# All values first, the linear projections as pairs of quarter sums, and pooling as the fill of the attention

## The chip, the cores and the metric

The kernel runs on one core of one Trainium2 chip. The core's engines are TensorE (PE, matrix products; PEld is its loading of weights), VectorE (DVE), ScalarE (ACT), GpSimd (POOL) and SyncE (SP, which here issues the DMA transfers). Each engine works through a queue of its own in order and waits on semaphores for the others. SBUF is the memory from which they read, PSUM the memory into which PE writes. The metric is the device time of one execution in microseconds: a median of several runs. One further execution is recorded by the profiler, and its own time is the span.

## The reference

One layer of a hybrid block on a sequence of 1024 tokens of width 1024, led by 16 meta tokens, all in float32. Shortened:

```
u  = rmsnorm(h, norm_mix)                          # h: 16 meta tokens + 1024 tokens
a, q, k, v, r, lr, ga, gb = split(u @ w_in)        # 512, 256, 256, 512, 512, 16, 1024, 1024 columns
p   = for group g of 4 (128 columns each): trailing mean of a over 2, 4, 8, 16 tokens, minus a
y_a = ((p @ w_pool_mix, group by group) * pool_scale) @ w_pool_out
log_a = log_sigmoid(lr @ w_gate_up + b_gate) / 16
o   = gla_chunked(q / 8, k, v, log_a)              # 4 heads, keys of 64, values of 128, chunks of 64 tokens:
      scores[t, s] = sum_k q[t,k] k[s,k] exp(-|b[t,k] - b[s,k]|)   # b: running sum of log_a in the chunk
      o = scores @ v + (q * exp(b)) @ S            # S: state, decayed and added to, chunk by chunk
y_b = (rmsnorm(o, gla_norm) * silu(r)) @ w_gla_out
m   = sigmoid(ga) * y_a + sigmoid(gb) * y_b
h   = h + m @ w_out
h   = h + square(relu(rmsnorm(h) @ w_ff1)) @ w_ff2          # 1024 -> 4096 -> 1024
out = rmsnorm(h)[16:]
```

## The kernel before, in words

A product of two float32 matrices is made of three matmuls on rounded parts (type fp32r): each operand is split into a high part (ACT copies it) and a low part (the operand minus its high part, on DVE or POOL); `mm3` then adds high x high, high x low and low x high into one PSUM bank (lines L250, L251, L252). The normed tokens lie transposed, channels over the 128 partitions, in the high parts `TH` and the low parts `TL`, one array per half of the tokens (512 each, the first with the 16 meta tokens). They are filled in the start stage: eight tiles of 128 tokens are loaded, normed, transposed by PE (L238) and split, and PE also forms each tile's values v for the first two heads, 24 matmuls of 256 or 272 columns a tile.

A block of 128 columns of w_in is projected as 8 x 3 matmuls for each half of the tokens (`project`): 48 matmuls of 512 columns a block, 96 for two; a and k also need the meta tokens, and so three pieces, 72 matmuls. Its weights come by the ring `W1`: a raw load, a high part by ACT (L75), a low part (L76) by DVE, or in the attention by POOL; two blocks are held.

After the start, a table in the code sets an order of pooling and gate blocks: a blocks (`a_block`), mix groups (`mix_block`: DVE forms the running sums `s`, L458 and L461, splits them into `ph`, ACT L464 and DVE L465; PE multiplies them by the mixing weights `mw`; ACT L470 and DVE L471 scale and split the result into `pm`), gate blocks of ga, and four `ya_block`s (pm times w_pool_out, times the gate, to DRAM). A gate needs a logarithmic sigmoid: three ACT passes L479 to L481, DVE L482, and one more ACT pass.

Then `gla`, the attention, runs four units (two pairs of heads x two halves of the tokens). Each unit has an inner part, `inside` (log decay; then six levels, at each of which DVE and ACT grow the decayed keys and queries, L744 to L748, PE makes 64x64 scores, L712, and DVE copies a part of them under a mask, L775), and an outer part, `across` (states L801 and L807, outputs L814 and L824, the norm L833 to L838, PE's transposes L842, gating by r and splitting into `yg` L843 to L846). Both are generators that yield how long PE would have to wait; `pour` spends that time, multiplied by `PACE`, on the fill: blocks of wide matmuls for k, q, the values of the second two heads (`v_second`), r, gb, and w_gla_out on half 0 (`yb_block(j, 0)`). So PE's instructions alternate between small attention matmuls and wide fill, in an order that is written down when the program is made. DVE, ACT, POOL and SP are ordered by a scheduler, which may move an instruction within its engine but not past what it depends on.

After the attention come yb of half 1, the product with w_out, the first MLP layer, and the second. The first MLP layer already computes a pair of two blocks by seven products of quarters (two halves of the tokens x two halves of the channels) where eight would be the plain way: sums and differences of quarters are formed on DVE ahead of the products and behind them. Memory is two stacks, `left` and `right`; what lies over another array's memory must wait for that array's last reader.

Of the kernel before, what the change touches and what calls it, by code (L numbers as in the profile page):

```python
# [31 lines left out]
PACE, LEVEL = 1.62, 1.6  # L32
# [24 lines left out]
class Ring:  # L57


    def __init__(self, nc, raw, hi, lo, depth):  # L60
        self.nc, self.raw, self.hi, self.lo, self.depth = nc, raw, hi, lo, depth
        self.queue, self.loaded, self.done = [], 0, 0
        self.views = {}
        self.eng = nc.vector

    def top_up(self):
        while self.loaded < min(self.done + self.depth, len(self.queue)):
            ap = self.queue[self.loaded]
            s = self.loaded % self.depth
# [34 lines left out]
def kernel(  # L104
# [45 lines left out]
    r_dram = dp.tile([HEADS, 2, P, HALF], F32, name="r_dram")  # L150
    h_dram = dp.tile([8, P, D], F32, name="h_dram")
# [5 lines left out]
    small = left.push("small", [P, 152], F32)  # L157
    small_at = [0]

    def tiny(n):  # L160
        a = small_at[0]
        small_at[0] += n
        assert small_at[0] <= 152
        return small[:, a : a + n]
# [7 lines left out]
    lrT_meta = left.push("lrT_meta", [16, 16], F32)  # L172
# [9 lines left out]
    MH, ML = ([a.rearrange("p k c -> p (k c)")[:, : KT * HALF].rearrange("p (k c) -> p k c", k=KT) for a in t] for t in (TH, TL))  # L182
# [47 lines left out]
    def transposed(u, half, at, tags=("ms",), to=None):  # L230
        rows = u.shape[0]
        th, tl = (t[half] for t in to or (TH, TL))
        if rows == P:
            for j in range(2):
# [4 lines left out]
                split_from_psum(th[:, 4 * j : 4 * j + 4, at : at + P], tl[:, 4 * j : 4 * j + 4, at : at + P], b)  # L239
        else:  # L240
# [38 lines left out]
    def enqueue(steps):  # L279
        for ring, aps, _ in steps:  # L280
            if ring:
# [23 lines left out]
    def buffer(key, depth, size=HALF):  # L305
        S[key] = left.push(key, [P, depth, size], F32)
# [25 lines left out]
    def v_tile(i, t):  # L332
# [16 lines left out]
        else:  # L349
            act.activation(S["v"][i][:, t], b[:, :256], ACT.Copy)  # L350
# [13 lines left out]
    S["v"] = [left.push("v0", [P, NC, 2 * P], F32)]  # L364
    left0 = left.mark()

    def start():
# [8 lines left out]
        S["vw"] = [right.push("vw0", [P, 2, KT, VP], F32R)]  # L376
# [5 lines left out]
        for t in range(8):  # L382
# [9 lines left out]
            if t == 0:  # L392
# [11 lines left out]
        v_tile(0, 7)  # L404
# [13 lines left out]
    def pool_open():  # L418
        left.pop_to(left0)
        buffer("a", 2, SEQ + META)  # L420
        buffer("s", 2, SEQ + META)
        right.pop_to(0)
        S["vw"].append(right.push("vw1", [P, 2, KT, 256], F32R))
        S["pm"] = right.push("pm", [P, 2, 4, SEQ], F32R)
        S["ph"] = right.push("ph", [P, 2, SEQ], F32R)
        mw = S["mw"] = right.push("mw", [P, 2, 4, P], F32R)
        r = raw.load(w_pool_mix.rearrange("g c e -> c g e"), 4 * P).rearrange("p (g e) -> p g e", g=4)
        act.activation(mw[:, 0], r, ACT.Copy)
        pool.tensor_tensor(mw[:, 1], r, f32(mw[:, 0]), ALU.subtract)
        buffer("t1", 2)  # L430
        buffer("g", 6)
        buffer("o", 2)
        raw.lend(left.push("raw2", [P, D], F32))

    step(one, pool_open)
# [3 lines left out]
    def a_block(g):  # L439
# [9 lines left out]
        return fn  # L449

    def mix_block(g):
        def fn():
# [13 lines left out]
            for tag, c in zip(("ms", "sc"), halves()):  # L466
                b = bank(tag)
# [4 lines left out]
                yield  # L472
# [3 lines left out]
    def sigmoid(b):  # L476

        t = nxt("t1")
        act.activation(t, b, ACT.Abs)  # L479
        act.activation(t, t, ACT.Exp, scale=-1.0)  # L480
        act.activation(t, t, ACT.Ln, bias=1.0)  # L481
        dve.scalar_tensor_tensor(t, b, 0.0, t, ALU.min, ALU.subtract)  # L482
        return t

    gates = {}

    def ga_block(d):
        def evac(b, half, at, n):
            t = sigmoid(b)
            g = gates[d, half] = nxt("g")  # L490
            act.activation(g, t, ACT.Exp)

# [863 lines left out]
```

## Time and profile before

| what | value |
| --- | --- |
| median of 3 runs | 1275.84 us (1275.65 to 1278.02) |
| span of the profiled execution | 1273.1 us, 2.7 us below the median |
| PE busy | 1237.9 us, 97% |
| DVE busy | 763.8 us, 60% |
| ACT busy | 592.5 us, 47% |
| POOL busy | 88.0 us, 7% |
| DMA | 164.92 MB, mean 130 GB/s |
| start stage | 0 to 57.9 us |
| pooling and gate blocks | 57.9 to 240.8 us |
| attention with fill | 240.8 to 520.7 us |
| rest (yb of half 1, output product, MLP) | 520.7 to 1273.1 us |

The stages are cut where PE starts on the first instruction of the next. A busy share is an average over stages with different limits; for what a change in one stage is worth the stage itself is looked at. Matmuls overlap in PE, so the mean duration of one in a row of the profile is longer than the distance from one to the next; the distance is had from a stretch of time and the number of matmuls in it. An idle time of an engine is put down to what it waited for last.

### The profile page before, as it was taken

The numbers are of one execution on the slowest core, as the hardware profiler recorded it, in microseconds if no ns is written. First come the engines' busy times: TensorE is split into PE (matmuls) and PEld (weight loads), VectorE is DVE, ScalarE is ACT, GpSimd is POOL, SyncE is SP. The second block draws the span as 40 slices with busy tenths as digits, with TensorE's granted clock in tenths as the row PEclk, the third lists the DMA queues.
The fourth block names the chain that finished last, engine by engine and source line by source line (L and its number), as shares of the span: only waits on it lengthen the run. The fifth ranks groups of instructions, "written<-read, shape, count | busy, mean of one in ns | idle before, by whom it ended". The sixth has DMA issues, their size and how long they took to land.

```text
span 1273.1 us, 17984 instructions
## 1 busy us (share of the span) xinstructions
PE 1237.9 (97%) x6895; PEld 1019.3 (80%) x6895; DVE 763.8 (60%) x1265; ACT 592.5 (47%) x1029; POOL 88.0 (7%) x48
## 2 busy tenths in 40 slices
PE   5999999999999999999999999999999999999997
PEld 4988888888778788778878888888878788888776
DVE  6446222251456554652787766766774877887686
ACT  6334334342465654431665545545553444444544
POOL 1000001000111112720000000000000000000000
PEclk9999999999999999999999999999999999999999
DMA  7111223210123324880235444445469863333532
GB/s 238 49 33 50 83 80 104 66 34 17 51 84 92 111 82 157 292 277 35 84 109 164 149 144 162 149 143 164 157 209 360 286 233 107 97 93 90 170 90 89
DMA packets 138103, 164.92 MB, mean 130 GB/s; under 512 B 10368, under 2 KB 82832, under 8 KB 138016
## 3 DMA queue, kind: packets, MB, share of 16 engines
q1 hardware_dynamic: 138016, 163.76, 40.1%
q8 instruction: 54, 0.88, 0.3%
q14 instruction: 33, 0.27, 0.1%
HBM read 115.50 MB, written 48.23 MB: 129 GB/s over the span
## 4 chain that ended last, share of the span: by engine, by line
PE 87%; DVE 5%; DMA 3%; ACT 2%; POOL 1%; issue 1%; SPq 0%; ACTq 0%; DVEq 0%
PE b_mm L250 13%; PE b_mm L251 13%; PE b_mm L252 13%; PE b_o L252 8%; PE b_o L251 8%; PE b_o L250 8%; PE b_y L250 3%; PE b_y L252 3%; PE b_y L251 3%; PE b_sc L250 2%; PE b_sc L252 2%; PE b_z L250 2%; PE b_sc L251 2%; PE b_z L252 2%; PE b_z L251 2%; PE b_sc L712 1%
## 5 line engine op out<-in xcount | busy, mean ns | idle before, releaser
L250 PE MATMUL b_mm<-th,w1h 128*128 128x512 f32 (+1 forms) x496 | 187.8, 379 | 0.0
L251 PE MATMUL b_mm<-tl,w1h 128*128 128x512 f32 (+1 forms) x496 | 185.0, 373 | 0.0
L252 PE MATMUL b_mm<-th,w1l 128*128 128x512 f32 (+1 forms) x496 | 184.4, 372 | 0.0
L250 PEld LDWEIGHTS b_mm<-th,w1h 128*128 128x128 f32 x496 | 93.4, 188 | 20.7 <-issue 3.4
L252 PEld LDWEIGHTS b_mm<-th,w1l 128*128 128x128 f32 x496 | 93.7, 189 | 16.9
L251 PEld LDWEIGHTS b_mm<-tl,w1h 128*128 128x128 f32 x496 | 93.5, 189 | 15.5
L75 ACT ACTIVATE w1h<-raw 128x1024 fp32r<-128x1024 f32 x40 | 42.4, 1059 | 87.6 <-PE b_mm L251 79.3
L482 DVE SCALAR_TENSOR_TENSOR t<-b_mm,t 128x512 f32<-128x512 f32 x40 | 27.6, 689 | 87.1 <-ACT t L481 87.1
L250 PE MATMUL b_o<-w1h 128*128 128x512 f32 x192 | 75.2, 392 | 2.7 <-DVE h L1179 1.7
L251 PE MATMUL b_o<-w1l,w1h 128*128 128x512 f32 x192 | 75.0, 391 | 1.2 <-DVE w1l L1033 1.2
L252 PE MATMUL b_o<-w1h,w1l 128*128 128x512 f32 x192 | 75.0, 391 | 0.1
L1032 ACT ACTIVATE w1h<-raw 128x512 fp32r<-128x512 f32 x88 | 54.7, 624 | 43.7 <-PE b_sc L251 14.1
L76 POOL TENSOR_TENSOR w1l<-raw,w1h 128x1024 fp32r<-128x1024 f32 x22 | 53.5, 2432 | 269.5 <-ACT w1h L75 269.5
L1033 DVE TENSOR_TENSOR w1l<-raw,w1h 128x512 fp32r<-128x512 f32 x88 | 60.2, 684 | 11.9 <-ACT w1h L1032 11.9
L1227 DVE TENSOR_TENSOR bt<-w,w 128x512 f32<-128x512 f32 x80 | 54.7, 684 | 2.4 <-DMA w<-in_w_ff_dram 2.4
L1032 ACT ACTIVATE w1h<-bt 128x512 fp32r<-128x512 f32 x45 | 28.3, 630 | 57.1 <-issue 33.5
L76 DVE TENSOR_TENSOR w1l<-raw,w1h 128x1024 fp32r<-128x1024 f32 x18 | 22.7, 1260 | 52.7 <-ACT w1h L75 52.2
L251 PE MATMUL b_mm<-wo,th 128*128 128x512 f32 x128 | 50.1, 391 | 1.3 <-DVE wo L913 1.3
L250 PE MATMUL b_sc<-th,w1h 128*128 128x512 f32 x128 | 50.5, 394 | 0.8 <-ACT u2p L1151 0.8
L250 PE MATMUL b_mm<-wo,th 128*128 128x512 f32 x128 | 50.7, 396 | 0.4 <-ACT wo L912 0.4
L251 PE MATMUL b_o<-fxl,fxh 128*128 128x512 f32 x128 | 50.0, 391 | 0.7 <-DVE small L211 0.7
L251 PE MATMUL b_z<-tl,w1h 128*128 128x512 f32 x128 | 49.9, 390 | 0.4 <-DVE tl L975 0.4
(294 smaller groups left out, 3073.6 us busy)
## 6 DMA issues: line engine op xcount, KB each, us to landing
hf_dram<-h SPq DMA_DIRECT2D x112, 256.0 KB, 2.1
raw<-hf_dram SPq DMA_DIRECT2D x112, 256.0 KB, 2.7
raw<-in_w_in_dram SPq DMA_DIRECT2D x32, 512.0 KB, 4.2
w<-in_w_ff_dram SPq DMA_DIRECT2D x64, 256.0 KB, 5.0
rawx<-in_w_ff_dram SPq DMA_DIRECT2D x16, 512.0 KB, 4.3
raw<-in_w_ff_dram SPq DMA_DIRECT2D x16, 512.0 KB, 4.1
xs<-in_x_dram SPq DMA_DIRECT2D x8, 512.0 KB, 5.7
ma_dram<-o SPq DMA_DIRECT2D x16, 256.0 KB, 2.0
```

The costliest lines, as they stand in the source:

```text
L75: self.nc.scalar.activation(hi, raw, ACT.Copy)
L76: self.eng.tensor_tensor(lo, raw, hi.bitcast(F32), ALU.subtract)
L250: pe.matmul(ps, ah, bh, start=first and i == 0, stop=False, skip_group_check=more)
L251: pe.matmul(ps, ah, bl, start=False, stop=False, skip_group_check=more)
L252: pe.matmul(ps, al, bh, start=False, stop=last and i == n - 1, skip_group_check=more)
L482: dve.scalar_tensor_tensor(t, b, 0.0, t, ALU.min, ALU.subtract)
L712: pe.matmul(b[to, e, j], kk[r, s], qq[r, s], start=True, stop=True, tile_position=(e * CH, u * CH))
L1032: act.activation(hi, a, ACT.Copy)
L1033: dve.tensor_tensor(lo, a, f32(hi), ALU.subtract)
L1227: dve.tensor_tensor(bt, w, S["w2"][q[3:]][:, i], ALU.add if q[2] == "+" else ALU.subtract)
```

## The change

*Start.* The weights of all four heads' values are loaded in the start stage, and both halves of the values are formed there, tile by tile, and written to DRAM (`v_dram`). ACT copies each transposed tile once more, in plain float32, into `xr`.

*k and the quarter sums.* `proj_open` forms from `xr` the four sums and differences of input quarters that the seven products need (DVE, one on POOL), and splits them. Meanwhile PE does the two k blocks, whose results go to DRAM.

*Pairs.* q (one pair of blocks), r (two), gb (four) and ga (four) are computed in one stage, `pairs_of_projections`, 11 pairs of seven products with 12 matmuls each, by the functions that the first MLP layer uses (`sums_order`, `sums_weights`, `split`: renamed and moved up). All results go to DRAM.

*Attention.* `gla` begins after that, with the first 10 us of fill poured in ahead of it (`OPENING`) and a `PACE` of 1.0. Its fill is now the pooling branch: four a blocks, four mix groups, four ya blocks, and, as before, yb on half 0. The a blocks are the last readers of `TH` and `TL`; `pm`, `ph`, the sums `s` and `mw` lie over these. k, q, v, r and the gates are read back from DRAM. `across` waits, where the order is made, until the mix groups are written down ("yg"), and a yb block of half 0 until that half's outputs are.

What follows the attention is as before. Lines of the changed kernel are numbered differently: `mm3` is L256 to L258, the sums L712 and L715, the split L719 and L725, the growth of keys and queries L910 and L912, the scores L880, the masked copies L941, the outputs L978 and L988, the norm's transposes L1006.

```diff
-PACE, LEVEL = 1.62, 1.6
+PACE, LEVEL, OPENING = 1.0, 1.6, 10.0
...
+                c = half * HALF + at - OFF[half]
+                act.activation(S["xr"][:, 4 * j : 4 * j + 4, c : c + P], b, ACT.Copy)
...
-            act.activation(S["v"][i][:, t], b[:, :256], ACT.Copy)
+            o = nxt("vo")
+            act.activation(o, b[:, :256], ACT.Copy)
+            nc.sync.dma_start(v_dram[i, t], o)
...
+                load_vw(1)
...
+            if t > 0:
+                v_tile(1, t - 1)
         transposed(um, 0, 0)
+        v_tile(0, 7)
+        v_tile(1, 7)
...
+    def proj_open():
+
+        left.pop_to(base)
+        right.pop_to(1)
+        S["t"] = [tuple(left.push(f"t{i}{k}", [P, 4, HALF], F32R) for k in "hl") for i in range(4)]
+        buffer("t1", 2)
+        buffer("o", 3)
+        piece = lambda half, j: S["xr"][:, 4 * j : 4 * j + 4, half * HALF : (half + 1) * HALF]
+        b11, b21, b12, b22 = (piece(h, j) for h in range(2) for j in range(2))
+
+        def parts(i, a, eng=dve):
+            hi, lo = S["t"][i]
+            act.activation(hi, a, ACT.Copy)
+            eng.tensor_tensor(lo, a, f32(hi), ALU.subtract)
+
+        dve.tensor_tensor(b11, b12, b11, ALU.subtract)
+        parts(0, b11)
+        pool.tensor_tensor(b12, b22, b12, ALU.subtract)
+        dve.tensor_tensor(b22, b22, b11, ALU.subtract)
+        parts(1, b22)
+        dve.tensor_tensor(b21, b21, b22, ALU.subtract)
+        parts(2, b12, pool)
+        parts(3, b21)
+
+    step(one, proj_open)
...
+    PAIRS = [(c + 2 * i * P, put, 2 * i) for c, n, put in (
+        (C_Q, 1, put_q), (C_R, 2, put_r), (C_GB, 4, put_gate(gb_dram)), (C_GA, 4, put_gate(ga_dram)),
+    ) for i in range(n)]
...
+    def pairs_of_projections():
+        load = lambda i, u: load_block(w_in, i, u, PAIRS[i][0])
...
+        plain = lambda half, j: tuple(t[half][:, 4 * j : 4 * j + 4, OFF[half] : OFF[half] + HALF] for t in (TH, TL))
+        x = {"P1": plain(0, 0), "P2": plain(0, 1), "P5": S["t"][0], "P3": plain(1, 1)}
+        x.update(zip(("P6", "P7", "P4"), S["t"][1:]))
+        xb, zb = {}, {}
+        left_over = 7 * len(PAIRS)
+        W1.shift = 1
+        for p, i, (ah, al) in ahead(sums_weights(len(PAIRS), load), 3):
+            bh, bl = x[p]
+            if p in ("P1", "P2"):
+                b = xb[i] = bank("sc") if p == "P1" else xb[i]
+            elif p in ("P5", "P3"):
+                b = zb[i] = bank("z") if p == "P5" else zb[i]
+            else:
+                b = bank("y")
+            more = p in ("P2", "P3")
+            mm3(b, 4, lambda k: (ah[:, k], al[:, k]), lambda k: (bh[:, k], bl[:, k]), first=not more, more=more)
+            left_over -= 1
+            if left_over == 2:
+                raw.back()
+                enqueue(rest)
+                W1.top_up(1)
+            u2, u3 = S["u2p"][:, i % 2], S["u3p"][:, i % 2]
+            put, d = PAIRS[i][1:]
+            if p == "P1":
+                act.activation(u2, b, ACT.Copy)
+            elif p == "P2":
+                put(d, 0, xb.pop(i))
+            elif p == "P6":
+                dve.tensor_tensor(u2, b, u2, ALU.add)
+            elif p == "P7":
+                dve.tensor_tensor(u3, b, u2, ALU.add)
+                c = nxt("c")
+                dve.tensor_tensor(c, zb[i], u3, ALU.add)
+                put(d + 1, 1, c)
+            elif p == "P4":
+                c = nxt("c")
+                dve.tensor_tensor(c, b, u3, ALU.add)
+                put(d + 1, 0, c)
+            elif p == "P3":
+                c = nxt("c")
+                dve.tensor_tensor(c, zb.pop(i), u2, ALU.add)
+                put(d, 1, c)
+            yield
+
+    step(one, pairs_of_projections)
...
+    def pool_open():
+        left.pop_to(left_ff)
+        S["pm"] = left.push("pm", [P, 2, 4, SEQ], F32R)
+        S["ph"] = left.push("ph", [P, 2, SEQ], F32R)
+        buffer("s", 2, 1056)
...
-    a_ = lambda g: step(one, a_block(g), W1, [w_cols(C_A + g * P)])
-    m_ = lambda g: step(one, mix_block(g))
-    g_ = lambda d: step(one, ga_block(d), W1, [w_cols(C_GA + d * P)])
-    y_ = lambda d: step(one, ya_block(d), W1, [rows4(w_pool_out, d)])
-    for f, i in (
-        (a_, 0), (a_, 1), (m_, 0), (a_, 2), (m_, 1), (a_, 3), (m_, 2), (g_, 0), (m_, 3), (g_, 1),
-        (y_, 0), (g_, 2), (g_, 3), (y_, 1), (g_, 4), (g_, 5), (y_, 2),
-    ):
-        f(i)
-    step(one, lambda: load_vw(1))
-    for f, i in ((g_, 6), (g_, 7), (y_, 3)):
...
-    def v_second():
-        for t in range(9):
-            v_tile(1, t)
-            yield 24 * 256 / 2400
...
+            while not h and ("o", 0) not in done:
+                yield "wait"
...
-        step(fill, k_block(p), W1, [w_cols(C_K + p * P)])
-        told(("k", p))
-        step(fill, q_block(p), W1, [w_cols(C_Q + p * P)])
-        told(("q", p))
-        if p == 0:
-            step(fill, v_second)
-            step(fill, yg_open)
-            told("v")
-    for h in range(4):
-        step(fill, r_block(h), W1, [w_cols(C_R + h * P)])
-        told(("r", h))
-    for d in range(8):
-        step(fill, gb_block(d), W1, [w_cols(C_GB + d * P)])
...
+    for g in range(4):
+        step(fill, a_block(g), W1, [w_cols(C_A + g * P)])
+    step(fill, pool_open)
+    for g in range(4):
+        step(fill, mix_block(g))
+    step(fill, yg_open)
+    told("yg")
+    for j in range(4):
+        step(fill, ya_block(j), W1, [rows4(w_pool_out, j)])
+    step(fill, merged_open)
     for j in range(4):
         step(fill, yb_block(j, 0), W1, [rows4(w_gla_out, j)])
...
-        while "v" not in done or ("r", 2 * p + 1) not in done:
+        while "yg" not in done:
...
-                if cost is None:
+                if cost is None or cost == "wait":
+                    owed[0] = 0.0
...
-        while ("k", 0) not in done:
-            next(filler)
+        pour(OPENING)
```

More of the change, by code (lines that the diff above doesn't have):

```diff
@@ L437, with load_v @@
+    def load_v(half):
+        for p in range(2):
+            nc.sync.dma_start(S["v"][:, p], v_dram[p, 4 * half : 4 * half + 4].rearrange("t p c -> p t c"))
+    step(rest, gla_open)
     pooled = {}
@@ L795, in across @@
         yield 1.6
-        while p and "v" not in done:
-            yield 1.0
         kv = two("m2").rearrange("p u (j c) -> p u j c", j=4)
@@ L882, in gla @@
             pass
-    step(one, gla)
+    step(rest, gla)
     def merge_open():
@@ L915, in load_wo @@
         return fn
-    step(one, merge_open)
+    step(rest, merge_open)
     def wo1_open():
@@ L1307 @@
     for fn in (ff_layers, ff2_open, ff2):
-        step(one, fn)
-    for ring, aps, fn in one:
-        if fn is gla:
-            enqueue(fill)
-        elif ring:
-            ring.queue.extend(aps)
+        step(rest, fn)
+    enqueue(one)
     with tc.manual_schedule(engines={mybir.EngineType.PE}):
-        for _ in drive(one):
-            pass
+        for steps in (one, rest):
+            for _ in drive(steps):
+                pass
     banks()
```

387 lines of the change are left out of this document (204 added, 183 removed).

## The prediction

> **What bounds the kernel now.** I read the page first: share of each engine, the 40 slices, the chain that ended last.
>
> ```profile
> span 1273.1 us, 17984 instructions
> PE 1237.9 (97%) x6895; PEld 1019.3 (80%) x6895; DVE 763.8 (60%) x1265; ACT 592.5 (47%) x1029; POOL 88.0 (7%) x48
> PE   5999999999999999999999999999999999999997
> PE 87%; DVE 5%; DMA 3%; ACT 2%; POOL 1%; issue 1%; SPq 0%; ACTq 0%; DVEq 0%
> ```
>
> TensorE (PE) is busy in every slice but the first and last, and is 87% of the chain. So a matmul removed is worth its spacing, and a microsecond in which PE must wait for another engine is lost whole. The span is 1273.1 us, the median 1275.84: I add 2.7 us to a span. Next the view by stretches of time, cut at the stages (start of PE's first block; the pooling and gate blocks; the attention with its fill; yb of half 1 and the output product) and at some places inside them:
>
> ```profile
> core 0: us, PE busy (x) PEld busy (x) DVE busy (x) ACT busy (x) POOL busy (x), PEclk, DMA share, GB/s
> 0.00:57.90 57.90, 41.65 (x299) 39.12 (x300) 35.07 (x74) 31.13 (x71) 7.78 (x10) 0.97 0.54 157
> 57.90:240.80 182.90, 182.90 (x890) 154.02 (x890) 66.71 (x76) 71.65 (x112) 4.82 (x2) 1.00 0.23 68
> 240.80:520.70 279.90, 277.31 (x2480) 226.47 (x2479) 133.84 (x251) 139.09 (x231) 54.10 (x24) 0.99 0.28 85
> 674.58:756.56 81.98, 81.98 (x362) 67.57 (x360) 57.41 (x90) 40.87 (x69) 0.00 (x0) 1.00 0.48 156
> 272.91:275.88 2.97, 2.97 (x25) 2.83 (x25) 1.92 (x3) 0.63 (x1) 0.00 (x0) 1.00 0.00 0
> 28.90:32.30 3.40, 0.29 (x4) 0.08 (x2) 3.36 (x4) 1.06 (x3) 1.65 (x2) 0.96 0.50 108
> 32.30:35.40 3.10, 3.10 (x14) 3.10 (x15) 3.03 (x10) 1.70 (x5) 0.00 (x0) 0.50 0.46 138
> ```
>
> From 57.9 to 520.7 us PE has no idle time to speak of: what the change removes there it gains, what it adds it pays. The fourth row is a stretch of the first MLP layer, already computed by the seven quarter-sum products: 30 products of 12 matmuls in 81.98 us, 2.733 us a product, **0.2277 us a matmul** of 512 columns. The last two rows show a second price of a wait: after 3.4 us with PE idle its granted clock was 0.50 for 3.1 us, so about 1.5 us more are lost.
>
> **1. The pairs.** q, r and both gates are 22 blocks of 48 matmuls; as 11 pairs they are 11 x 7 x 12 = 924 matmuls of the same shape instead of 1056 (a pair: 84 for 96). 132 x 0.2277 = **30.1 us less**. The products feed ACT and DVE at the rate that the fourth row shows: per pair (19.1 us of PE) DVE is busy 13.4 and ACT 9.5 there; the logarithmic sigmoid adds to ACT four times the four passes below (2.48 us), for what the first layer does with its results. ACT then has about 15 of 19.1 us: it fits. I take nothing for it; +1 at most at the first pair, before the rings are full.
>
> ```profile
> 412.09 0.58 ACT L479 ACTIVATE t<-b_mm 128x512 f32<-128x512 f32 x1
> 412.70 0.64 ACT L480 ACTIVATE t<-t 128x512 f32<-128x512 f32 x1
> 413.37 0.63 ACT L481 ACTIVATE t<-t 128x512 f32<-128x512 f32 x1
> 414.76 0.63 ACT L590 ACTIVATE o<-t 128x512 f32<-128x512 f32 x1 [0.76 <-DVE t L482]
> ```
>
> The Trainium skill ("TensorE: Matmul & The Clock Gate", section "Back-to-back issue gap") gives 131 ns for each of a sustained stream of weight loads and matmuls of 512 columns. By that figure the 132 matmuls would save an estimated 17.3 us, not 30.1. The stretch above, with such a stream and a full clock, shows 228 ns, and decides.
>
> **2. Values in the start.** Nine tiles of 24 matmuls leave the attention (2.97 us each by the row 272.91 to 275.88, so 26.7 us) and join the start. There PE is busy 41.65 of 57.9 us, so some idle time could take them; but they need a second weight load and its split on ACT and POOL in the stage where PE already waits for those engines, and each transposed tile now gets one more ACT copy. From the 3.4 us gap I allow up to 2.4 either way: **0**. The quarter sums of the inputs (DVE, ACT, POOL) lie beside the k blocks: k needs none of them.
>
> **3. The pooling sums.** Now pooling is fill inside the attention. The sums, `s`, lie in the memory of the transposed inputs, which the a blocks read. PE's order around the first pooling product (ph, the split pooled sums, times mw), before:
>
> ```order
> L252 MATMUL b_mm<-th_133,w1l 128x512
> L250 MATMUL b_ms<-ph,mw 128x512
> L251 MATMUL b_ms<-ph,mw 128x512
> L252 MATMUL b_ms<-ph,mw 128x512
> L250 MATMUL b_sc<-ph,mw 128x512
> L251 MATMUL b_sc<-ph,mw 128x512
> L252 MATMUL b_sc<-ph,mw 128x512
> L250 MATMUL b_mm<-th_125,w1h 128x264
> ```
>
> and now (b_sc<-n are scores of the attention):
>
> ```order
> L258 MATMUL b_mm<-th_137,w1l 128x512
> L880 MATMUL b_sc<-n_2774 64x64 x16
> L256 MATMUL b_mm<-ph,mw 128x512
> L257 MATMUL b_mm<-ph,mw 128x512
> L258 MATMUL b_mm<-ph,mw 128x512
> L256 MATMUL b_mm<-ph,mw 128x512
> L257 MATMUL b_mm<-ph,mw 128x512
> L258 MATMUL b_mm<-ph,mw 128x512
> L880 MATMUL b_sc<-n_2770 64x64 x16
> L256 MATMUL b_mm<-ph,mw 128x512
> ```
>
> Before, a wide a or gate block stood between two mix groups; now all four stand behind the last matmul of a block 3, with two score groups as their only company. DVE's order there, with what each row waits for:
>
> ```order
> L712 TENSOR_TENSOR s<-a 128x1024 [waits PE_49]
> L941 COPY_PREDICATED scc<-mask,b_sc 128x512 [waits DVE_49,PE_49]
> L715 SCALAR_TENSOR_TENSOR s<-s,a 128x1024 [waits DVE_49]
> L910 TENSOR_TENSOR n_2774<-n_2770,ends 128x8x2x32
> L912 TENSOR_TENSOR f<-n_2770,ends 128x8x64 [waits Activation_49]
> L719 TENSOR_TENSOR ph<-s,ph 128x512 [waits Activation_49] x2
> L712 TENSOR_TENSOR s<-a 128x1026
> L725 SCALAR_TENSOR_TENSOR pm<-b_mm,small,pm 128x512 [waits Activation_49] x2
> ```
>
> The first sum itself waits for PE. The four groups have 1 + 2 + 3 + 4 = 10 running sums (L712), 4 closing ones (L715), 8 splits (L719) and 8 of the results (L725). Their rows before:
>
> ```profile
> 109.27 1.23 DVE L458 TENSOR_TENSOR s<-a 128x1038 f32<-128x1038 f32 x1
> 110.53 3.77 DVE L458 TENSOR_TENSOR s<-s 128x1036 f32<-128x1036 f32 x3
> 114.33 1.23 DVE L461 SCALAR_TENSOR_TENSOR s<-s,a 128x1024 f32<-128x1024 f32 x1
> 116.25 1.29 DVE L465 TENSOR_TENSOR ph<-s,ph 128x512 fp32r<-128x512 f32 x2
> L471 DVE SCALAR_TENSOR_TENSOR pm<-b_sc,small,pm 128x512 fp32r<-128x512 f32 x3 | 2.2, 741 | 0.0
> 406.68 0.73 DVE L775 COPY_PREDICATED scc<-mask,b_sc 128x512 f32<-128x512 uint8 x1
> 383.12 2.67 DVE L744 TENSOR_TENSOR n<-n,mix 128x512 f32<-128x512 f32 x1
> 382.85 2.38 POOL L76 TENSOR_TENSOR w1l<-raw,w1h 128x1024 fp32r<-128x1024 f32 x1 [11.64 <-ACT w1h L75]
> L744 DVE TENSOR_TENSOR n<-n,ends 128x512 f32<-128x512 f32 x16 | 10.8, 676 | 0.0
> ```
>
> 14 x 1.26 + 8 x 0.65 + 8 x 0.74 = 28.8 us, and the attention's own rows in the queue (two COPY_PREDICATED, two steps of growth, one of the norm, 0.7 to 1.2 each) some 4: 32.5. PE has 24 mix matmuls (5.5) and two score groups (0.6 each) meanwhile, so it stands about **26 us**. Two things move this. An operation of DVE on two SBUF operands took 2.67 instead of 0.68 us while POOL subtracted a weight's low part: ya's first low part (2.4) falls into the sums, +2. A part of the last splits and of the attention's rows may run behind PE's restart: 0 to -4, I take -1.5. Half the clock afterwards, as in the row 32.30 to 35.40: +1.5. 26 + 2 - 1.5 + 1.5 = **+28**, bounds 22 and 33.5 (all of the 4 off and no loss of clock; nothing off and 5.5 for POOL and the clock, with 2 more where `s` waits for ACT's high parts). Before, the same sums cost PE nothing: it is busy 182.90 of 182.90 us there.
>
> **4. The tail.** The last attention unit, PE, before (b_m_4199, transposes L842; 16 groups of three yb matmuls between, then yb again):
>
> ```order
> L824 MATMUL b_m_4199<-W,mix 64x128 x9
> L250 MATMUL b_mm<-yg_2497,w1h 128x512
> L251 MATMUL b_mm<-yg_2497,w1h 128x512
> L252 MATMUL b_mm<-yg_2497,w1l 128x512
> L250 MATMUL b_mm<-yg_2497,w1h 128x512
> ```
>
> and now:
>
> ```order
> L258 MATMUL b_mm<-yg_3652,w1l 128x512
> L978 MATMUL b_m_4669<-v,scc 64x128 x16
> L988 MATMUL b_m_4669<-W,mix 64x128 x4
> L988 MATMUL b_m_4669<-S,mix 64x128
> L988 MATMUL b_m_4669<-W,mix 64x128
> L988 MATMUL b_m_4669<-S,mix 64x128
> L988 MATMUL b_m_4669<-W,mix 64x128 x9
> L1006 MATMUL b_m_4714<-ident,mix 128x128 x8
> L256 MATMUL b_mm<-yg_2736,w1h 128x512
> ```
>
> The fill is used up before the last outputs, so nothing stands between them and the norm's transposes (L1006), nor between these and the first product that needs their result (yb of half 1). What PE covered before, in an earlier unit:
>
> ```profile
> 404.49 1.03 ACT L833 ACTIVATE mix<-b_m 128x1024 f32<-128x1024 f32 x1 [3.38 <-PE b_m L824]
> 405.55 1.22 DVE L836 TENSOR_REDUCE small<-mix 128x8 f32<-128x1024 f32 x1 [3.15 <-ACT mix L833]
> 409.73 1.22 DVE L838 TENSOR_TENSOR mix<-b_m,small 128x1024 f32<-128x1024 f32 x1
> 416.37 1.23 DVE L843 TENSOR_TENSOR mix<-b_m,mix 128x1024 f32<-128x1024 f32 x1 [1.65 <-PE b_m L842]
> 417.63 1.06 ACT L845 ACTIVATE yg<-mix 128x1024 fp32r<-128x1024 f32 x1
> ```
>
> From 404.5 to 410.95 are 6.5 us with other work in DVE's queue, about 5.4 without. After L1006 come 1.23 + 1.06 for the high part and as much as 1.2 for the low one, of which six matmuls on the other heads hide 1.4: 2. Sum 7.4 to 8.5, up to 1.5 more for the clock, and down to 5 if the two waits overlap other rows: **+8**.
>
> **5. The rest of the attention.** Scores, state and outputs are the same instructions, with less fill beside them (696 matmuls, x 0.2277 = 158 us). What could be new are waits in its chains. Their rows in the whole stage before:
>
> ```profile
> PE b_ms L793 <- DVE gB L689: 1.3, 1, 1.3
> PE b_ms L659 <- ACT metab L660: 1.2, 2, 0.6
> PE b_sc L712 <- DVE scc L775: 0.2, 1, 0.2
> L775 DVE COPY_PREDICATED scc<-mask,b_sc 128x512 f32<-128x512 uint8 x24 | 17.7, 739 | 17.7 <-PE b_sc L712 17.6
> ```
>
> It was DVE that waited for PE. I take the first two rows once more, and 1.5 for k and q now coming back by DMA before the first scores: **+4**, bounds 0 and 8. From yb of half 1 on nothing changes: 0.
>
> **Sum.** -30.1 + 0 + 28 + 8 + 4 = +9.9: span 1283.0, time **1286**. With all low ends: -31 - 2.4 + 22 + 5 + 0 = -6.4, so 1269; with all high ends: -29 + 2.4 + 33.5 + 10 + 8 = +24.9, so 1301. Their own range, since not all ends come together: 1277 to 1297.
>
> **Rivals.** *A, the other side: the sums are hidden.* If DVE could run the groups 0 to 2 as their a blocks end, as it did before, only group 3 (7.6 us of sums and splits) would stand, and with the mix matmuls of the others in front some 5 us: -30.1 + 5 + 8 + 4 = -13.1, **1263**. For: before, exactly that held. Against: the first L712 waits for PE's last a matmul, since `s` lies over the transposed inputs. It turns faster as soon as the stall is under 18 us. Chance 0.17, with the milder case of a short stall and tail. *B, the pairs are bound by ACT.* The results' sigmoids are queued on ACT in front of the next weights' high parts; if each pair waited 1.5 us, that is two L479 rows and more, +16.5: **1302**. For: ACT at 15 of 19.1; against: three products are prepared ahead. Chance 0.08. *C, the attention starves.* With a pace of 1.0 for 1.62 each of the 24 levels might leave PE waiting for one copy under the mask (0.74): +17.8, **1304**. For: less fill per level; against: the third row above. Chance 0.1. *D, the pairs save less:* a matmul removed is worth 131 ns, so they give 17.3: **1298**. Only the page speaks for it; 0.02. The forecast itself has 0.63.
>
> The range that should hold it is 1271 to 1301. About 0.2% (2.5 us) can be told from no change. Faster: A and the low edge of my own, 0.22; the same 0.09; slower 0.69.
>
> **What would show it.** In the profile after: 924 matmuls of pairs with no gap, 2.73 a product; a wait of PE for ph or pm of 20 us and more, right after the fourth a block, with DVE busy throughout and a lower granted clock behind it; a wait of 5 us or more at L1006 and a shorter one in front of yg_2736; the start ending near 84.5 (57.9 + 26.7). I am wrong if PE stays busy at the mix products, if the start grows by under 20, or if the waits at L941 and L880 appear.

## The result, and the profile after

The changed kernel takes **1304.04 us** (median of 4 runs, 1303.27 to 1305.24), the kernel before 1275.74 us beside it. The ratio is 1.0224, 95% interval 1.0210 to 1.0239: slower, by 28 us, where 10 were forecast with a range up to 1301. The sign was right, the size almost three times the forecast.

The page of the changed kernel, its lines that answer to those shown before (the fourth is the granted TensorE clock in tenths, slice by slice):

```profile
span 1302.2 us, 18212 instructions
PE 1225.4 (94%) x6763; PEld 1005.7 (77%) x6763; DVE 881.4 (68%) x1433; ACT 635.2 (49%) x1115; POOL 77.4 (6%) x42
PE   5999999999993989699999999999999999999997
PEclk9999999999995989799999999999999999999999
PE 77%; DVE 8%; ACT 2%; issue 2%; DMA 2%; SPq 0%; POOL 0%; ACTq 0%; DVEq 0%; POOLq 0%
```

PE has 12.5 us less of busy time and the span is 29.1 us longer. Slices 13 to 17 of 40 show where: PE idle, and its clock down, in the attention. The stretches of time of the changed kernel, cut at its stages (start; k blocks; first pair; other pairs; attention up to the end of the last a matmul; the mix groups, up to the first ya matmul; ya; yb of half 0 and the tail, up to yb of half 1):

```profile
core 0: us, PE busy (x) PEld busy (x) DVE busy (x) ACT busy (x) POOL busy (x), PEclk, DMA share, GB/s
0.00:82.60 82.60, 66.76 (x512) 63.88 (x513) 42.02 (x78) 50.78 (x100) 17.24 (x13) 0.98 0.47 139
82.60:105.40 22.80, 22.80 (x148) 20.84 (x146) 11.97 (x8) 6.45 (x12) 4.01 (x1) 1.00 0.30 82
105.40:121.60 16.20, 13.22 (x55) 9.83 (x54) 5.50 (x8) 5.69 (x11) 0.00 (x0) 1.00 0.21 62
121.60:320.80 199.20, 199.20 (x873) 163.35 (x872) 135.96 (x209) 136.37 (x236) 0.00 (x0) 1.00 0.36 105
320.80:388.30 67.50, 64.54 (x759) 54.29 (x757) 39.67 (x84) 32.22 (x62) 7.30 (x3) 0.97 0.37 118
388.30:425.50 37.20, 14.69 (x90) 8.90 (x90) 33.87 (x42) 13.08 (x22) 4.62 (x2) 0.62 0.09 29
425.50:505.00 79.50, 74.52 (x820) 59.02 (x819) 53.17 (x97) 27.09 (x42) 10.41 (x5) 0.94 0.55 177
505.00:551.50 46.50, 33.86 (x293) 26.36 (x291) 31.03 (x48) 14.75 (x23) 20.31 (x12) 0.82 0.49 157
```

The pairs run without a gap after the first. In the four attention rows PE is idle for 43.1 us (67.5 - 64.54, 37.2 - 14.69, 79.5 - 74.52, 46.5 - 33.86), against 2.6 us in the attention before. (The 34.8 us that some expectations below give for the gap at the mix groups end at 423.2, inside the fourth group, with five mix matmuls still to come. Up to the first ya matmul it is 37.2.) The granted clock falls there too. PE's busy time times the part of the clock that was not granted, summed over slices of half a microsecond, is 18.3 us in these rows, and 1.7 in the attention before. This loss is called half clock below, as the clock is mostly 0.50 where it is not full.

A count of the work agrees roughly. The fill is 288 a matmuls (four blocks of 11.3 us when nothing lies between) and 24 + 192 + 96 of 512 columns at 0.2277 us, 116 us in all. The attention's own matmuls took 51.6 us before (277.31 busy, less 224.0 of fill: k 22.4, q 21.9, v 26.7, r 43.7, gb 87.4, yb 21.9; less 1.7 of half clock). Together that is 168 us, and PE is busy for 187.6, which is 20 more. What PE waited for, in the whole changed kernel:

```profile
PE b_mm L256 <- ACT ph L718: 21.0, 4, 6.5
PE b_m L1006 <- DVE mix L1002: 8.5, 3, 5.2
PE b_sc L880 <- DVE scc L941: 7.2, 3, 3.8
PE b_sc L256 <- ACT u2p L617: 2.0, 2, 1.0
PE b_sc L256 <- ACT o L485: 1.0, 1, 1.0
```

The first row is the mix groups. The second holds the tail (5.2) and two earlier units' norms, the third the levels of the attention, the last two the first pair.

The budget in spans, by stage: start +24.7 (82.6 for 57.9), values out of the attention -26.7, the pairs' stage -25.1 (215.4 for 1056 x 0.2277), k +0.4, idle time in the attention +43.1, half clock +18.3, less what the attention had of both before (2.6 idle, 1.7 half clock), and 1.7 less behind 551.5 (750.7 for 752.4). That is +28.7; measured are 29.1.

### The profile page after: what moved, and what is told of

It is laid out like the page before. It is cut to its first block, busy times and chain, and to the rows that moved or that the text cites. A ratio compares the mean times of both kernels' runs of the same rounds, so it can differ in the third digit from the quotient of the medians.

```text
span 1302.2 us, 18212 instructions
## 1 busy us (share of the span) xinstructions
PE 1225.4 (94%) x6763; PEld 1005.7 (77%) x6763; DVE 881.4 (68%) x1433; ACT 635.2 (49%) x1115; POOL 77.4 (6%) x42
## 3 DMA queue, kind: packets, MB, share of 16 engines
q1 hardware_dynamic: 149632, 180.58, 43.1%
## 4 chain that ended last, share of the span: by engine, by line
PE 77%; DVE 8%; ACT 2%; issue 2%; DMA 2%; SPq 0%; POOL 0%; ACTq 0%; DVEq 0%; POOLq 0%
PE b_o L257 7%; PE b_o L258 7%; PE b_o L256 7%; PE b_y L256 6%; PE b_y L257 6%; PE b_y L258 6%; PE b_mm L256 5%; PE b_mm L257 5%; PE b_mm L258 5%; PE b_z L257 4%; PE b_z L258 4%; PE b_z L256 4%; PE b_sc L256 3%; PE b_sc L257 3%; PE b_sc L258 3%
## 5 line engine op out<-in xcount | busy, mean ns | idle before, releaser
L525 ACT ACTIVATE w1h<-fs 128x512 fp32r<-128x512 f32 x81 | 51.2, 632 | 63.9 <-PE b_y L257 39.8
L256 PE MATMUL b_o<-w1h 128*128 128x512 f32 x192 | 75.4, 393 | 2.7 <-DVE h L1274 1.7
L258 PE MATMUL b_o<-w1h,w1l 128*128 128x512 f32 x192 | 75.3, 392 | 0.1
L526 DVE TENSOR_TENSOR w1l<-fs,w1h 128x512 fp32r<-128x512 f32 x81 | 55.6, 687 | 24.7 <-ACT w1h L525 24.7
L256 PE MATMUL b_sc<-mh,w1h 128*128 128x512 f32 x128 | 50.1, 392 | 0.8 <-ACT u2p L1246 0.8
L256 PE MATMUL b_mm<-wo,mh 128*128 128x512 f32 x128 | 50.7, 396 | 0.0
L257 PE MATMUL b_z<-ml,w1h 128*128 128x512 f32 x128 | 49.9, 390 | 0.4 <-DVE ml L1134 0.4
L258 PE MATMUL b_mm<-wo,ml 128*128 128x512 f32 x128 | 50.2, 392 | 0.0
L257 PE MATMUL b_mm<-wo,mh 128*128 128x512 f32 x128 | 50.2, 392 | 0.0
L258 PE MATMUL b_o<-fxh,fxl 128*128 128x512 f32 x128 | 50.2, 392 | 0.0
L257 PE MATMUL b_sc<-ml,w1h 128*128 128x512 f32 x128 | 50.0, 391 | 0.0
L256 PE MATMUL b_o<-fxh 128*128 128x512 f32 x128 | 49.9, 390 | 0.0
L258 PE MATMUL b_sc<-mh,w1l 128*128 128x512 f32 x128 | 49.8, 389 | 0.0
L258 PE MATMUL b_z<-mh,w1l 128*128 128x512 f32 x128 | 49.8, 389 | 0.0
L256 PE MATMUL b_z<-mh,w1h 128*128 128x512 f32 x128 | 49.8, 389 | 0.0
```

The source lines that it names most:

```text
L256: pe.matmul(ps, ah, bh, start=first and i == 0, stop=False, skip_group_check=more)
L257: pe.matmul(ps, ah, bl, start=False, stop=False, skip_group_check=more)
L258: pe.matmul(ps, al, bh, start=False, stop=last and i == n - 1, skip_group_check=more)
L525: act.activation(hi, a, ACT.Copy)
L526: dve.tensor_tensor(lo, a, f32(hi), ALU.subtract)
```

## The experiments

Two theories stood at first. One: the excess over the forecast comes from **too little fill** in the attention, so that single levels and norms stand bare. The other: **DVE**, which now has the pooling beside the attention, is too full or is held up, and more or other fill would not help. All ratios are to the kernel before, run beside each group (1274.98, 1274.36 and 1275.09 us in the three groups). Gains and losses against the changed kernel are differences of medians; taken from the ratios they come out up to 2 us different.

### The pairs undone (e5_plain)

```diff
...
-    step(one, pairs_of_projections)
+    def plain_block(put, d):
+        return lambda wb: project(wb, MAIN, lambda b, half, at, n: put(d, half, b))
+    for c, put, d in PAIRS:
+        for u in range(2):
+            step(one, plain_block(put, d + u), W1, [w_cols(c + u * P)])
+    step(one, lambda: enqueue(rest))
```

> q, r and both gates as 22 plain blocks of 48 matmuls instead of 11 pairs of 84, in the same place, all else as changed (the quarter sums are still formed and not used). Theory (a matmul removed is worth its spacing of 0.2277 us, less 4 us of waits that the first pairs show): 132 more matmuls cost 26 to 30 us, time 1330 to 1334. Rival (a removed matmul is worth 131 ns, 17.3 us, less the waits): 1317 to 1321.

Measured: 1335.06 us (1330.87 to 1335.43), ratio 1.0467 [1.0450, 1.0485]. That is 31 us above the changed kernel in the medians, a microsecond above the expected 1334, and 26.9 in the spans of the two profiled executions (1329.1 and 1302.2). ACT's copy of the first a block's second half, first in the changed kernel, then in this one, stands 30.3 us later. Below it are the stretch of the plain blocks and PE's first a matmul in this run:

```profile
333.51 0.58 ACT L689 ACTIVATE a<-b_mm 128x512 f32<-128x512 f32 x1
```

```profile
363.77 0.59 ACT L635 ACTIVATE a<-b_mm 128x512 f32<-128x512 f32 x1
105.40:347.60 242.20, 242.20 (x1055) 197.71 (x1053) 59.94 (x69) 122.18 (x186) 0.00 (x0) 1.00 0.33 101
351.23 0.39 PE L256 MATMUL b_mm<-th,w1h 128*128 128x264 f32 x1 [3.46 <-DVE t L480]
```

Not all of that is the pairs. The plain blocks take PE 242.2 us without a wait, where the pairs' stage took 215.4 (16.2 + 199.2): 26.8 us less. Most of the rest is one wait of 3.5 us at the first a matmul, which only this variant has. Without the 3.0 us of waits in the first pair the pairs save 29.8 us, 0.226 us for each of the 132 matmuls. The rival of 131 ns each falls.

### The pooling sums moved, and left out (e1_sums, e11_nosums)

The first writes the sums behind each a block, over buffers that nobody uses there. The second has only the last part of the edit: the sums go, and the mix groups read a, so the pooled means are missing from its result.

```diff
 def a_block(g):
             yield from project(wb, WITH_META, evac)
...
+            two_s = [S[n].rearrange("p a b -> p (a b)") for n in ("t1", "o")]
+            cur, k, i = a, 1, 0
+            while k < w:
+                c = META - (w - 2 * k)
+                dst = two_s[i % 2]
+                dve.tensor_tensor(dst[:, c:e], cur[:, c:e], cur[:, c - k : e - k], ALU.add)
+                cur, k, i = dst, 2 * k, i + 1
+            dve.scalar_tensor_tensor(a[:, META:e], cur[:, META:e], 1.0 / w, a[:, META:e], ALU.mult, ALU.subtract)
...
 def mix_block(g):
...
-            cur, k = a, 1
-            while k < w:
...
-            dve.scalar_tensor_tensor(pp[:, :SEQ], cur[:, META:e], 1.0 / w, a[:, META:e], ALU.mult, ALU.subtract)
+            pp = pooled[g][:, META : SEQ + META]
```

> The pooling sums lie over the buffers t1 and o, which nobody uses during the a blocks, and each group's sums stand right behind its a block; the closing sum is written over a itself. All arithmetic is the same, and PE's order too. Theory (the stall of 34.8 us at the mix groups is DVE's chain of sums, released by the last a matmul): the 14 sums of 1.26 us leave the stall, 17.6 us, which leaves 8 splits and 8 results on DVE, about 11 us; the time falls by 15 to 22 us, to 1282 to 1289. Rival (DVE's total load sets the stage's length, wherever the sums stand): PE waits for the masked copies in the a blocks instead, and the time falls by under 8 us.

Measured: 1297.26 us (1296.67 to 1298.65), ratio 1.0180 [1.0165, 1.0195]: 7 us less than the changed kernel, not 15 to 22.

> The changed kernel without the 14 operations of the trailing sums: the mix groups take the plain a instead (so the pooled means are left out of the result). Splits, products and everything else stay. Theory (the gap of 34.8 us at the mix groups is DVE's chain, of which the sums are 17.6 us): the gap falls to 15 to 18 us, and as nothing is moved elsewhere, the time falls by 17 to 22, to 1282 to 1287; the difference to the run with early sums (7 us) is what the moved sums cost in the a blocks. Rival (the gap is held by something else, ACT's parts, PE's turn-round, POOL): the time falls by less than 10.

Measured: 1280.99 us (1280.67 to 1285.6), ratio 1.0059 [1.0040, 1.0077]: 23 us less (21 by the ratios). The stretch from the last a matmul to the first ya matmul, 37.2 us in the changed kernel, is now 19.0, with 17.05 of DVE:

```profile
387.90:406.90 19.00, 11.59 (x90) 6.86 (x90) 17.05 (x27) 12.38 (x22) 3.65 (x2) 0.82 0.19 56
```

So the stall is DVE's chain, as forecast: without the sums the gap is 18.2 us shorter, and some 4 go behind it, most of it half clock. But moved under the a blocks the sums cost a large part of what they cost where they stood: of the 23 us only 7 are gained. The last copy of an a block by ACT shows it, at 389.52 in the changed kernel and at 396.08 with early sums:

```profile
389.52 0.57 ACT L689 ACTIVATE a<-b_mm 128x512 f32<-128x512 f32 x1
```

```profile
396.08 0.57 ACT L689 ACTIVATE a<-b_mm 128x512 f32<-128x512 f32 x1
351.96 3.03 DVE L698 TENSOR_TENSOR t<-a 128x1026 f32<-128x1026 f32 x1
351.52 2.38 POOL L76 TENSOR_TENSOR w1l<-raw,w1h 128x1024 fp32r<-128x1024 f32 x1 [15.91 <-ACT w1h L75]
PE b_sc L880 <- DVE scc L941: 11.3, 4, 4.1
320.80:394.90 74.10, 66.10 (x759) 55.73 (x757) 49.70 (x93) 32.30 (x62) 7.31 (x3) 0.95 0.31 97
```

6.6 us are lost before the mix groups begin (the gap itself is 25.6 us instead of 37.2). One early sum took 3.03 us instead of 1.22 beside POOL, and PE waited 4.1 us for the masked copy behind it. Group 3's sums (four and one) are still in the gap, since a block 3 is the last. The rival forecast this time, but its reason, that DVE's total load sets the length, does not fit the last row: in the a blocks DVE is busy for 49.7 of 74.1 us, 67%, and PE is idle for 8.0. What costs is where the sums stand in DVE's queue: a group's sums come in one run, and the rows for which PE waits stand behind or between them. Whether another order of that queue would hide them was not tried.

### The portions of the fill, and the pace (e2_fine, e3_pace)

```diff
 def ya_block(j):
-                    mm3(b, 4, lambda i: (hi[:, i, w], lo[:, i, w]), lambda i: (pm[:, 0, i, c], pm[:, 1, i, c]))
+                    for k in range(4):
+                        mm3(
+                            b, 1, lambda i: (hi[:, k, w], lo[:, k, w]),
+                            lambda i: (pm[:, 0, k, c], pm[:, 1, k, c]), first=k == 0, last=k == 3,
+                        )
+                        yield 3 * 512 / 2400
...
-                    yield 12 * 512 / 2400
```

> The ya blocks give their fill in portions of 3 matmuls instead of 12; the total fill and the pace are the same. Theory (levels are left without any fill, because one portion of 12 pays for more than a level, and PE then waits for the masked copy and falls to half clock): the waits of L880 for L941 (7.2 us) fall under 3, the time by 4 to 10 us, to 1294 to 1300. Rival (these waits come from DVE's load and from POOL holding DVE up, not from the portions): the waits stay within 2 us of 7.2 and the time within 2.5 us of 1304.

Measured: 1297.97 us (1295.69 to 1300.5), ratio 1.0184 [1.0168, 1.0201], 6 us less (5 by the ratios), as the theory of fill has it. The waits of the scores (L880, here L884) are down from 7.2 to 3.7, not quite under 3:

```profile
PE b_sc L884 <- DVE scc L945: 3.7, 3, 2.8
PE b_m L1010 <- DVE mix L1006: 8.0, 2, 5.2
```

```diff
-PACE, LEVEL, OPENING = 1.0, 1.6, 10.0
+PACE, LEVEL, OPENING = 1.62, 1.6, 10.0
```

> PACE 1.62 as in the kernel before, else the changed kernel. If the fill is enough and only its pace is too low, the waits of L880 go and the time falls by 5 to 15 us. If the total fill is the limit, it runs out earlier: the waits move from the ya blocks to the levels behind them and to the last unit's norm, and the time stays within 5 us of 1304 or rises by up to 25.

Measured: 1323.0 us (1321.57 to 1324.0), ratio 1.0377 [1.0359, 1.0394], 19 us more. The fill runs out earlier, and the waits gather at the norms of the last units:

```profile
PE b_m L1006 <- DVE mix L1002: 21.0, 3, 10.2
PE b_sc L880 <- ACT mix L924: 4.5, 2, 2.3
PE b_sc L880 <- DVE scc L941: 2.0, 2, 1.0
```

The total of fill is the limit, and the low pace is the better way to divide it.

### The low parts on DVE (e4_dvelow)

```diff
 def gla_open():
-        W1.eng = pool
```

> The changed kernel with one edit: in the attention the low parts of the weights are subtracted by DVE (1.2 us each) instead of POOL (2.4 us each). Theory (the waits of L880 for L941 in the ya and yb blocks, 3.8 and 3.0 us, are those in which one DVE operation lasts 2.5 to 3 us because POOL subtracts at that moment): these waits fall to under 1.5 in all, the DVE row that took 3.37 us in the mix stall takes 1.2, the time falls by 5 to 10 us, to 1294 to 1299. Rival (DVE is simply too full, 8 of 10 tenths; the subtractions on it make it fuller): the time stays within 2.5 us or rises.

Measured: 1299.94 us (1299.31 to 1303.63), ratio 1.0201 [1.0178, 1.0224], 4 us less in the medians, 3 by the ratios; this interval and that of the changed kernel overlap, so the gain is not certain. That POOL holds DVE up is seen in the changed kernel's timeline, at its longest wait for a masked copy:

```profile
473.90 2.50 DVE L923 TENSOR_TENSOR mix<-n,ends 128x256 f32<-128x256 f32 x1
476.33 0.71 DVE L941 COPY_PREDICATED scc<-mask,b_sc 128x512 f32<-128x512 uint8 x1
476.94 0.41 DVE L923 TENSOR_TENSOR mix<-n,ends 128x256 f32<-128x256 f32 x1
473.77 2.35 POOL L76 TENSOR_TENSOR w1l<-raw,w1h 128x1024 fp32r<-128x1024 f32 x1 [15.89 <-ACT w1h L75]
```

The same operation takes 2.50 us while POOL subtracts and 0.41 us after it; the masked copy stands behind it in DVE's queue, and of the 3.77 us that PE waits for that copy some 2.1 are this delay. With the subtractions on DVE the waits of the scores are 5.7 us instead of 7.2, where the theory wanted under 1.5:

```profile
PE b_sc L879 <- DVE scc L940: 5.7, 4, 2.5
```

So POOL explains a small part of the waits only.

### More fill (e12_twice)

```diff
 def ya_block(j):
-                    mm3(b, 4, lambda i: (hi[:, i, w], lo[:, i, w]), lambda i: (pm[:, 0, i, c], pm[:, 1, i, c]))
+                    for _ in range(2):
+                        mm3(b, 4, lambda i: (hi[:, i, w], lo[:, i, w]), lambda i: (pm[:, 0, i, c], pm[:, 1, i, c]))
+                        yield 12 * 512 / 2400
...
-                    yield 12 * 512 / 2400
```

> The changed kernel, with each product of the ya blocks computed twice into the same bank (the second overwrites the first): 192 matmuls more, 43.7 us of PE, with no work for DVE, ACT or POOL. Theory (the attention is short of fill after the mix groups, and PE's waits and half clock there, some 18.5 + 8 us with the tail, are idle time that any fill would use): 20 to 28 us of the 43.7 are absorbed, time 1320 to 1328. Rival (the waits come from DVE's load and its hold-ups by POOL, which more fill does not thin out): under 12 absorbed, 1336 and more.

Measured: 1333.59 us (1331.48 to 1336.37), ratio 1.0466 [1.0447, 1.0485]. 43.7 us of matmuls cost 29.5, so 14 are absorbed, between the two forecasts. The stall at the mix groups is what it was (37.2 us), the last norm costs next to nothing any more, and the scores still wait. The last two rows are the stretch from the first ya matmul to yb of half 1, in the changed kernel and in this one:

```profile
PE b_mm L256 <- ACT ph L718: 21.1, 4, 6.5
PE b_sc L881 <- DVE scc L942: 3.9, 3, 2.0
PE b_m L1007 <- DVE mix L1003: 0.5, 1, 0.5
425.50:551.50 126.00, 108.38 (x1111) 85.38 (x1109) 84.20 (x144) 41.85 (x64) 30.72 (x16) 0.90 0.53 170
424.40:582.00 157.60, 152.26 (x1332) 121.71 (x1331) 83.18 (x146) 44.80 (x66) 32.73 (x16) 0.98 0.41 129
```

In that stretch PE's idle time falls from 17.6 to 5.3 us, and its half clock, summed as above, from 10.0 to 2.7. So of the 27.6 us lost there fill that costs DVE nothing removes 19.6, with the same work for DVE (84.20 and 83.18 us busy). Some 4 come back behind it, where yb of half 1 now waits for DVE (2.0 us) and for its weights (twice 1.2). Behind the mix groups, then, most of the loss is shortage of fill, as the first theory has it. The stall at the mix groups is DVE's, and the extra fill, which stands behind it, leaves it alone.

### The tail, and four edits together (e10_hold_alone, e7_combo, e8_hold, e13_hold)

```diff
+    def tail():
+        while "tail" not in done:
+            yield "wait"
     for j in range(4):
+        if j == 3:
+            step(fill, tail)
         step(fill, yb_block(j, 0), W1, [rows4(w_gla_out, j)])
...
 def gla():
+            if u is None:
+                done.add("tail")
```

> The changed kernel with only the last yb block of half 0 held back for the last unit's outer part. Theory: the 5.2 us at the last L1006 go, with the half clock behind them, and 2 to 4 us of new waits come in the last unit's levels: 1298 to 1302. Rival (fill is short everywhere in the last unit): the waits at L880 and L978 there rise by 5 and more, and the time stays within 2.5 us of 1304.

Measured: 1303.34 us (1302.11 to 1306.02), ratio 1.0228 [1.0203, 1.0253], no difference; but PE's order at the last norm had not changed, so this tells nothing. (The held block is 24 matmuls, 5.5 us, not 48: yb of half 0 is 8 products of 12 matmuls in all.)

Next the early sums, the groups in the order 3, 2, 1, 0, ya's portions of 3, and the low parts on DVE in one kernel:

```diff
-    for g in range(4):
+    for g in (3, 2, 1, 0):
         step(fill, a_block(g), W1, [w_cols(C_A + g * P)])
     step(fill, pool_open)
-    for g in range(4):
+    for g in (3, 2, 1, 0):
         step(fill, mix_block(g))
```

> Four edits at once: the sums right behind each a block (as in the run with early sums), the groups in the order 3, 2, 1, 0, so that the longest sums come first and only 2 operations stand behind the last a matmul, ya's fill in portions of 3 matmuls, and the low parts on DVE. Theory (the stall is made of DVE's work that the last a matmul releases, and the early sums gained only 7 us because group 3's five sums still stood there and POOL held DVE up): the gap at the mix groups falls from 34.8 us to about 16 (8 splits and 8 results, 11 us, and the attention's own rows), the waits of L880 vanish, the time falls by 20 to 30 us against the changed kernel, to 1274 to 1284. Rival (the work moved fills DVE in the a blocks and comes back there): gain of 7 to 14, to 1290 to 1297.

Measured: 1294.18 us (1291.83 to 1296.01), ratio 1.0148 [1.0127, 1.0170]: 10 us less than the changed kernel, as the rival's time had it. The gap at the mix groups falls to 20.8 us (402.1 to 422.9), but the a blocks end 13.8 us later:

```profile
403.32 0.57 ACT L688 ACTIVATE a<-b_mm 128x512 f32<-128x512 f32 x1
PE b_sc L883 <- DVE scc L944: 6.5, 5, 2.9
PE b_ms L858 <- DVE metab L855: 4.6, 1, 4.6
PE b_ms L962 <- DVE gB L860: 3.1, 1, 3.1
```

PE now waits for DVE's rows of the attention among the sums, 4.6 us for a small one of the meta tokens, 3.1 for the decay. Here too DVE is not full: up to 402.1 us it is busy for 51.2 of 81.3 us, while PE is idle for 12.6. With the held-back block released as in the run above:

> As the run with four edits, and the last yb block of half 0 (48 matmuls, 10.9 us) is held back until the last unit's outer part. Theory (nothing covers the last norm, 5.2 us of waiting at L1006, 1.1 behind it and some 2 of half clock): 4 to 8 us less than that run, since some of the waits move to the last unit's levels. Rival (the fill taken from these levels is missed there as much): within 2.5 us of it.

Measured: 1293.96 us (1292.76 to 1296.13), ratio 1.0150 [1.0129, 1.0170]: no difference, for the same reason. Then released at the norm itself (the edit is against the run just told):

```diff
-            if u is None:
-                done.add("tail")
...
 def across(p, half):
+        if (p, half) == (1, 1):
+            done.add("tail")
         yield 6.0
```

> As the run with four edits, but the held-back yb block is let go only at the last norm (in the two runs with held-back fill it was let go at the beginning of the last outer part, and PE's order at the last norm came out unchanged, so they tested nothing). Now 24 matmuls stand ahead of the last transposes and the rest behind them. Theory (the tail is 8 us because nothing covers the norm): the 5.2 us at L1006 go with the half clock behind it, the state's chain costs 2 to 4 more in the same unit: 2 to 6 us under the run with four edits, 1288 to 1292. Rival (a shortage of fill only moves): within 2 us of 1294.

Measured: 1295.95 us (1293.78 to 1298.34), ratio 1.0168 [1.0152, 1.0184]: no gain. The last norm's wait is down from 5.2 to 0.55 us, and in its place PE waits 3.2 us for the state (L980), 1.1 more for its transposes and 2.0 for the split result:

```profile
PE b_m L987 <- DVE W L980: 3.2, 1, 3.2
PE b_mm L256 <- ACT yg L1020: 2.0, 1, 2.0
PE b_m L974 <- ACT mix L969: 1.1, 1, 1.1
```

The shortage moves. No version tried beats the kernel before; the one without the sums does not either.

## Why the prediction was wrong

**Pairs (-30.1): right in the mechanism**, and 3 to 5 us too good. The stage is 25.1 us shorter than 1056 matmuls at 0.2277, and 26.8 shorter than with the pairs undone; the low and high ends were -31 and -29. The first pair waits 3.0 us where +1 at most was allowed: its first products have to wait for ACT's copies (L617, L485) before the next may use the bank.

**Values in the start (0): right** within its bounds. The start ended at 82.6 us, forecast 84.5, so -2.0. The quarter sums lie beside the k blocks, where PE is busy 22.80 of 22.80 us.

**The pooling sums (+28): right**, in place, cause and size. In the gap PE is idle for 22.5 us and loses 6.7 to half clock, and 1.1 more behind it: 30.3, within the bounds of 22 and 33.5. The mean clock in it was 0.62. That POOL holds DVE up there showed too: the first sum took 3.37 us, the first closing one 1.67:

```profile
389.81 3.37 DVE L712 TENSOR_TENSOR s<-a 128x1024 f32<-128x1024 f32 x1
393.72 1.67 DVE L715 SCALAR_TENSOR_TENSOR s<-s,a 128x1024 f32<-128x1024 f32 x1
389.69 2.41 POOL L76 TENSOR_TENSOR w1l<-raw,w1h 128x1024 fp32r<-128x1024 f32 x1 [17.86 <-ACT w1h L75]
392.06 2.26 POOL L703 TENSOR_TENSOR mw<-raw,mw 128x512 fp32r<-128x512 f32 x1
```

Rival A rested on the sums being hidden under the a blocks. In the order tried it would have been wrong even where the memory allowed it: moved there, they brought 7 us of 23.

**The tail (+8): right.** 5.2 us at L1006, 1.1 behind it and some 1.7 of half clock, 8.0.

**The rest of the attention (+4, bounds 0 and 8): here it failed.** The prediction took two waits of the attention before once more and priced no shortage of fill. Idle time outside the gap and the tail is 43.1 - 22.5 - 5.4 = 15.2 us (0.9 of the tail's waits lie behind 551.5), half clock outside them 18.3 - 6.7 - 1.1 - 1.7 = 8.8; less 4.3 that the attention had before, +19.7. Of the 19 us by which the span missed (+29.1 for +9.9) this term is some 16, the pairs 5, the sums 2; the start and what follows the attention gave back some 4.

Two errors made the term too small. The fill was counted at 696 matmuls and 158 us; it is 600, and with a's narrower pieces 116 us, since half 0 of yb is 8 products of 12 and not 16. The attention before had 224 us. And the row that spoke against a shortage ("DVE waited for PE", 0.2 us at the scores) came from a stage with that ample fill and a DVE 48% busy (133.84 of 279.90 us); it could say nothing of one with half the fill and a DVE 68% busy (157.74 of 230.7). The sign that the prediction itself named came: waits of PE at L880 for L941, 7.2 us.

That the shortage is the larger part is shown by the ya products computed twice, which removed 19.6 of the 27.6 us lost behind the mix groups, the tail among them. Portions of 3 matmuls took 5 to 6 us, the low parts on DVE up to 4 (not certain). These effects overlap and do not add up to a full division of the term.

Rival C, the starved attention, had the mechanism nearest to this, a price of 17.8 and a time of 1304. Its form was not right: the waits are not at each of 24 levels, but at three levels, the norms of the last units and the state, with half clock behind several of them. That its time is the measured one is luck, since the pairs and the sums came out 5 and 2 us higher as well. It was given 0.1. The clock was priced at two places only, 1.5 us at the sums and up to 1.5 in the tail; the whole attention lost 18.3.

## What to carry to other kernels

Work that serves as cover has two sides: the time it fills on the engine that must not wait, and what it puts into the queues of the engines whose latency it should cover. Pooling brings 29 us of DVE with its 51 us of PE (four a blocks and 24 mix matmuls). Beside an attention that needs DVE itself, these rows stood in front of rows for which PE waited, though DVE was not full. Count, per stage, the fill that is left in matmuls, and look at what stands in each queue ahead of the awaited rows, before trading one fill for another. And a wait row near zero says only that the cover sufficed: when the cover is halved, price each chain bare, with the half clock that follows a wait.

## What the hardware showed unexpectedly

The half clock lasts as long as the gaps recur, and some microseconds longer. In the 37.2 us at the mix groups PE was busy for 14.69 us in short pieces, and the granted clock was 0.62 in the mean. From the second mix matmul on, matmuls that follow one another stand 0.43 us apart instead of 0.23, and the spacing of 0.23 returns at 427.9 us, 5.4 us after the last of the waits ended. Over the whole attention half clock cost 18.3 us, nearly as much as the 20.6 us of idle time outside that gap.
